# Sums of squares of loaded weight units, two to four slots later

## The chip, the cores and the metric

The kernel runs on one core of a Trainium2 chip. The metric is the time of one execution on the device in microseconds (us): 822.87 us, the median of 3 runs (822.29 to 823.02).

## The reference, cut to what matters

One decoder layer over 512 tokens of width 2048. The input is normalised and multiplied with a matrix of 2048 x 7168; its columns feed a convolution (value and gate), q, k and v of an attention, and two gates. Both branches meet in an output projection.

```python
h = rms_norm(x, norm_g)
z = h @ w_in
a_val, a_glu, a_gate, q, k, v, b_gate = jnp.split(z, SPLIT_POINTS, axis=-1)
...
y = jnp.concatenate([y_a, y_b], axis=-1) @ w_out
return x + y
```

All of it is computed in fp32; the kernel reaches that with three 16-bit products, from a high and a low part of each operand.

## The kernel before, in words

**Units and groups.** The weights are cut into groups of 512 columns, in the order of GROUPS: vg0, vg1, vg2, vg3 (value and gate of the convolution), q0, k0, v0, bg0, q1 and so on. A group of the input projection is four units of 512 rows (1 MB each): vg2 is units 8 to 11, vg3 12 to 15, q0 16 to 19, k0 20 to 23, v0 24 to 27, bg0 28 to 31, q1 32 to 35. The first two groups are computed in another way (exact_matmuls). Eight buffers (RING) hold raw units. When a unit is done with, the load of the unit eight further on is issued on SP's queue (load, L256).

**What is done to a unit.** A loaded unit is first measured (measure, L267): ScalarE (ACT) squares its 2048 columns and sums them (row_squares, L188). When the four units of a group are measured, `bound` (L192) makes the group's scale from the sums: a ones-matmul on TensorE, a reduce on VectorE (DVE), two small instructions on GpSimd (POOL), and, two slots later, two more on DVE. With the scale, ACT writes the high part of a weight in 16 bits and DVE the low part. Four buffers (PARTS) hold such parts, so a new part waits until TensorE is done with the part four before it.

**Two kinds of groups.** A plain unit is split whole (split_hi L296, split_lo L301), and takes eight slots of six matmuls over 512 columns. The three groups in SEVEN (vg3, q0, v0) are computed with seven products in place of eight, of blocks of half the columns, each product in four slots of twelve matmuls over 256 columns: 28 slots for four units (input_products, L1103). The seven products want the blocks a11, a22, a12 and a21 of the weights and four sums of them. The sums s2, s3 and s4 are made in the raw buffers by DMAs that POOL issues and that accumulate (`add`, L1119), s1 by DVE. For each product, in the order of `order`, `hi` puts the high part five slots and `lo` (L1125 and below) the low part four slots ahead of the product's slots, for each of two pairs of units. The products in order are a22, a11, a12, s3, s1, s2, s4 (in vg3 a11 is before a22); product n runs in slots 4n to 4n+3, pair 0 in the first two of them.

**What sets the order.** The program is written out slot by slot. `after(n, fn)` puts work on a calendar n ticks later; the clock counts eight ticks a unit, and in a group of seven it jumps one tick after every seven slots, since 28 slots stand for 32 ticks. What is due in a slot is issued before that slot's own parts, and both before its matmuls. Every engine runs its instructions in that order; one that waits holds up all behind it. DVE also carries the convolution, a few instructions a slot up to a pace (run_conv, L850).

**The squares.** In a group of seven, `lo` gives a raw buffer free when its last sums are split: in slots 12, 20, 20 and 22. It then loads the unit eight further on, and measures it MEASURE ticks later:

```python
raw.pop(i0 + j)
load(i0 + j + RING)
after(MEASURE, lambda j=j: measure(i0 + j + RING))
```

Before, with MEASURE = 8, the four squares of k0's units stand in slots 19, 27 and 27 of vg3 and slot 1 of q0; those of v0's units in the same slots of q0 and k0; those of q1's in the same slots of v0 and bg0. A plain unit measures the unit eight further on nine ticks after its own split: those of q0's units in slots 6 of unit 8, 3 of unit 9, 3 of unit 10 and 3 of unit 11, those of bg0's in slot 5 of unit 20 and slots 3 of units 21, 22 and 23. In slot 3 of units 11 and 23 `hi` also puts the first high part of the next group of seven, behind the square.

Of the kernel before, what the change touches and what calls it, by code (L numbers as in the profile page):

```python
# [27 lines left out]
RING = 8  # L28
# [24 lines left out]
SEVEN = (("vg", 3), ("q", 0), ("v", 0))  # L53
# [2 lines left out]
SUM_FROM = 58  # L56
SUM_STEP = 10
PACE_2 = 1480
MEASURE = 8
IN_W1 = [g for g in GROUPS if g[0] in ("vg", "q", "k", "v", "ag", "bg")]  # L60


# [22 lines left out]
def layer(ctx: ExitStack, tc: tile.TileContext, xt, w1, w2, w3, g_in, conv_w, conv_b,  # L85
# [34 lines left out]
    def after(n, fn):  # L120

        calendar.setdefault(clock[0] + max(n, 1), []).append(fn)
# [65 lines left out]
    def row_squares(src, acc, n, scale=1.0):  # L188
        with nc.allow_low_precision(reason="a bound"):
            A.activation(junk[:, :n], src, AF.Square, scale=scale, accum_out=acc)  # L190

    def bound(name, sums, done, top=TOP):  # L192


        bufs = 8 if name == "w" else 1
        scale = small.tile([P, 1], F32, name=f"{name}s", bufs=bufs)
        inv = small.tile([P, 1], F32, name=f"{name}i", bufs=bufs)
        n = sums.shape[-1]

        def sum_up():  # L200
            ps = s_ps.tile([P, S], F32, name="ps_s")
            T.matmul(ps[:, 0:n], ones16, sums, start=True, stop=True)
            V.tensor_reduce(scale, ps[:, 0:n], axis=AX.X, op=OP.add)
            G.tensor_scalar(scale, scale, 1e-30, 2.0 ** (-2 * top), op0=OP.max, op1=OP.mult)  # L204
            rsqrt(scale)

        def finish():
            pow2_floor(scale)
            V.reciprocal(inv, scale)
            done(scale, inv)  # L210

        after(2, sum_up)
        after(4, finish)
# [27 lines left out]
    units = []  # L241
# [14 lines left out]
    def load(i, cuts=(0, KU)):  # L256
        if i < len(units):
            w, g, p = units[i][:3]
            raw[i] = raw_pool.tile([P, KU, S], F32, name="wf")
            for a, b in zip(cuts, cuts[1:]):  # L260
                load_part(i, a, b)
# [5 lines left out]
    def measure(i):  # L267
        if n_exact <= i < len(units):
            group = units[i][3:]
            mine = of_group[group]  # L270
            j = mine.index(i)
            if group not in sums:
                sums[group] = small.tile([P, len(mine)], BF16, name="wsum")
                to_measure[group] = len(mine)
            row_squares(raw[i].rearrange("p k n -> p (k n)"), sums[group][:, j:j + 1], KU * S)
            to_measure[group] -= 1
            if not to_measure[group]:
                after(4, lambda: bound("w", sums.pop(group), lambda s, v: wscale.update({group: (s, v)}),
                                       TOP - (group[0] == "wa" or group in SEVEN)))
# [16 lines left out]
    def split_hi(i):  # L296
        if i < n_plain:
            parts[i] = [part_pool.tile([P, KU, S], F16, name=n, tag="part") for n in ("wh", "wl")]
            A.activation(parts[i][0], raw[i], AF.Copy, scale=wscale[units[i][3:]][0])  # L299

    def split_lo(i):  # L301
        if i < n_plain:
            wh, wl = parts[i]
            V.scalar_tensor_tensor(wl, raw.pop(i), wscale[units[i][3:]][0], wh, op0=OP.mult, op1=OP.subtract)
            load(i + RING)
            after(9, lambda: measure(i + RING))

    def split16(src, scale, name):

# [793 lines left out]
    def input_products(i0):  # L1103
# [23 lines left out]
        def lo(name, pair):  # L1127
# [3 lines left out]
            for j in range(4):  # L1131
                mine = ("s2", "s4") if j % 2 else ("s1", "s3")
                if all((n, j // 2) in done for n in mine) and all(m in free for m in range(j)) and j not in free:
                    free.add(j)
# [4 lines that stand above are left out]
# [153 lines left out]
    def startup(n):  # L1292

        s, second = divmod(n, 2)
        todo = []
        if not second:
            if s + 3 < KU * n_exact:
                todo += [lambda: exact_hi(s + 3), lambda: exact_lo(s + 3)]
            if s + 2 < KC:
                todo.append(lambda: split_x(s + 2))  # L1300
        if n == 0:
            for k in range(1, KC):
                after(4 + (k - 1) * 26 // 14, lambda k=k: square_x(k))
            for n in range(KC):
                after(NORM_FROM + n * (70 - NORM_FROM) // KC, lambda k=n // 2 + 4 * (n // 8) + 4 * (n % 2): norm_x(k))
            for j in range(8):
                after(SUM_FROM + SUM_STEP * j // 2, lambda j=j: sum_x(j))
            g = token_rsqrt(xacc, D, RMS_EPS, rstd, rrow)
            for m in (32, 33, 36):
                after(m, lambda: next(g, None))  # L1310
            for m, fn in ((21, x_consts), (40, score_consts), (37, u_consts)):
                after(m, fn)
            after(8 * n_exact - 4, lambda: split_hi(n_exact))
            after(8 * n_exact - 3, lambda: split_lo(n_exact))
        return todo
# [6 lines left out]
    for i in range(n_plain):  # L1322
        kind, g = group = units[i][3:]
        if group in SEVEN:
            if i == of_group[group][0]:
                plan = ahead.pop(i) + later
                later = []
                n_next = i + 4
                if units[n_next][3:] in SEVEN:
                    ahead[n_next] = input_products(n_next)  # L1330
                    plan += [(n + 28, fn) for n, fn in ahead[n_next] if n < 0]
                else:
                    plan = [(24, lambda: split_hi(n_next)), (25, lambda: split_lo(n_next))] + plan
                for n in range(28):
                    clock[0] = 8 * i + n + n // 7
                    for fn in due_now():
                        fn()
                    first = [fn for k, fn in plan if k == n]
                    for fn in first[:]:
                        if fn.__name__ != "matmuls":  # L1340
                            fn()
                    run_conv()
                    for fn in first:
                        if fn.__name__ == "matmuls":
                            fn()
                later = [(n - 28, fn) for n, fn in plan if n >= 28]
                if units[n_next][3:] not in SEVEN:
                    for n, fn in later:
                        after(8 * n_next + n - clock[0], fn)
                    later = []  # L1350
                if kind == "k":
                    attention(g)
            continue
        exact = i < n_exact
        if exact:
            order = [(None, None)] * 8
        else:
            order = [(m, hf) for m in range(4) for hf in range(2)]
            extra = [[] for _ in range(8)]
            if i == n_plain - 1:  # L1360
                for n, fn in seven_parts(0):
                    if n < 0:
                        extra[n].append(fn)
            if i + 1 < len(units) and units[i + 1][3:] in SEVEN:
                ahead[i + 1] = input_products(i + 1)
                for n, fn in ahead[i + 1]:
                    if n < 0:
                        extra[n].append(fn)
            else:
                extra[0].append(lambda: split_hi(i + 1))  # L1370
                extra[2].append(lambda: split_lo(i + 1))
            if i + 1 < len(units) and units[i + 1][3] == "wb":
                for m in range(2):
                    extra[4 * m].append(lambda m=m: fetch_res(2 * units[i + 1][4] + m))
# [77 lines left out]
```

## Time and profile before

| | |
|---|---|
| median of 3 runs | 822.87 us |
| the profiled execution | 823.61 us |
| its span, first to last instruction | 821.8 us |
| TensorE busy | 809.5 us, 98% |
| VectorE (DVE) busy | 706.4 us, 86% |
| ScalarE (ACT) busy | 553.9 us, 67% |
| GpSimd (POOL) busy | 140.3 us, 17% |
| granted clock of TensorE | full speed in all slices |

All times are us from the start of the span of one profiled execution. Matmuls are pipelined and their ends are modelled, so the start of one to the start of the next is their cost, not the recorded length. Idle time of an engine counts where another engine waits for it in the end. Lines are those of the kernel; many DVE instructions are recorded under one helper (L80), and are told apart by what they write and read: `ws` is a part in a group of seven, `wh` and `wl` the parts of a plain unit, `junk` the squares, `wf` a raw unit.

### The profile page before, as it was taken

Reading aid. Unit: us, or ns where it says so; the run is one execution under the profiler, and the core shown is the slowest. Engines: PE = TensorE matmul, PEld = TensorE weight load, DVE = VectorE, ACT = ScalarE, POOL = GpSimd, SP = SyncE. Lnnn points to the kernel's source line nnn. Section 1 sums busy time; section 2 is a strip of 40 time slices with the busy share of each in tenths; the row PEclk is TensorE's granted clock in tenths of the full one; section 3 lists DMA queues with packets and bytes.
Section 4 is the critical chain, followed back from the end, with each engine's and each line's share of the span. In section 5 each row is a group of like instructions: output and inputs, shape, how many; then the busy total and the mean of one; then the engine's idle time right before and its main releaser. Section 6 shows DMA issues by size and latency. Waiting matters only on the chain.

```text
span 821.8 us, 13494 instructions
## 1 busy us (share of the span) xinstructions
PE 809.5 (98%) x5271; PEld 501.3 (61%) x5271; DVE 706.4 (86%) x1181; ACT 553.9 (67%) x778; POOL 140.3 (17%) x159
## 2 busy tenths in 40 slices
PE   9999999999998999999999999999999999999998
PEld 6787645878644864444444444444444444788887
DVE  6768989968887979999999988997667798998985
ACT  6667687475744589577665849577688858766540
POOL 0001020413043600002304010001110002422420
PEclk9999999999999999999999999999999999999999
DMA  9852343995583873737474641636343377578752
GB/s 339 340 215 100 105 114 93 146 255 114 219 180 85 147 242 103 167 103 167 128 137 129 170 131 55 163 103 167 103 116 103 119 232 249 111 176 187 133 104 65
DMA packets 98625, 125.62 MB, mean 153 GB/s; under 512 B 62720, under 2 KB 83968, under 8 KB 89344
## 3 DMA queue, kind: packets, MB, share of 16 engines
q1 hardware_dynamic: 80800, 107.38, 42.2%
q0 software_dynamic: 17472, 17.30, 15.0%
q8 instruction: 41, 0.67, 0.3%
q14 instruction: 24, 0.20, 0.1%
q10 hardware_dynamic: 288, 0.07, 0.0%
HBM read 88.56 MB, written 4.19 MB: 113 GB/s over the span
## 4 chain that ended last, share of the span: by engine, by line
PE 71%; DVE 17%; DMA 5%; issue 3%; ACT 3%; POOL 1%; SPq 0%; ACTq 0%; DVEq 0%; POOLq 0%
PE ps_l L408 17%; PE ps_l L409 17%; PE ps_l L410 17%; PE ps_l L876 10%; DVE cv L80 6%; DMA wf<-w_dram 4%; DVE wl L80 3%; PE ps_s L410 2%; PE ps_s L408 2%; PE ps_s L409 2%; DVE ws L80 2%; PE ps_s L720 2%; PE ps_o L760 2%; DMA wf<-wf 1%; ACT junk L190 1%
## 5 line engine op out<-in xcount | busy, mean ns | idle before, releaser
L80 DVE SCALAR_TENSOR_TENSOR cv<-u,cw,cv 128x511 f32<-128x511 f32 (+14 forms) x240 | 162.4, 727 | 0.0
L190 ACT ACTIVATE junk<-wf 128x2048 uint8<-128x2048 f32 x68 | 129.2, 1900 | 26.6 <-DMA wf<-w_dram 26.3
L408 PE MATMUL ps_l<-x,wh 128*128 128x512 f16 x320 | 121.3, 379 | 0.3 <-DVE glu L80 0.3
L299 ACT ACTIVATE wh<-wf,ws 128x2048 f16<-128x2048 f32 x44 | 87.7, 1993 | 50.3 <-PE ps_l L409 50.3
L410 PE MATMUL ps_l<-x,wl 128*128 128x512 f16 x320 | 121.3, 379 | 0.0
L409 PE MATMUL ps_l<-x,wh 128*128 128x512 f16 x320 | 121.3, 379 | 0.0
L80 DVE SCALAR_TENSOR_TENSOR wl<-wf,ws,wh 128x2048 f16<-128x2048 f32 x45 | 105.6, 2346 | 8.9 <-ACT wh L299 8.9
L80 DVE SCALAR_TENSOR_TENSOR ws<-wf,ws 128x1024 f16<-128x1024 f32 x70 | 89.0, 1278 | 17.9 <-ACT ws L1125 15.6
L409 PE MATMUL ps_l<-wl,x 128*128 128x512 f16 x256 | 97.0, 379 | 0.5 <-DVE wl L80 0.5
L408 PE MATMUL ps_l<-wh,x 128*128 128x512 f16 x256 | 97.1, 379 | 0.0
L410 PE MATMUL ps_l<-wh,x 128*128 128x512 f16 x256 | 97.0, 379 | 0.0
L408 PEld LDWEIGHTS <-wh 128*128 128x128 f16 x480 | 47.0, 98 | 55.2 <-issue 3.5
L410 PEld LDWEIGHTS <-wl 128*128 128x128 f16 x480 | 46.9, 98 | 53.6 <-DVE wl L80 0.4
L409 PEld LDWEIGHTS <-wh 128*128 128x128 f16 x480 | 46.9, 98 | 50.4 <-issue 0.7
L876 PE MATMUL ps_l<-xr,wr 128*128 128x512 f32 x288 | 70.2, 400 | 0.1
L204 POOL TENSOR_SCALAR ws<-ws 128x1 f32<-128x1 f32 x22 | 9.3, 424 | 331.2 <-DVE ws L80 302.3
L876 PEld LDWEIGHTS ps_l<-xr,wr 128*128 128x128 f32 x288 | 54.5, 190 | 14.1 <-ACT xr L335 1.0
L410 PEld LDWEIGHTS <-x 128*128 128x128 f16 x352 | 34.4, 98 | 33.4 <-issue 2.0
L408 PEld LDWEIGHTS <-x 128*128 128x128 f16 x352 | 34.4, 98 | 32.4 <-issue 1.9
L409 PEld LDWEIGHTS <-x 128*128 128x128 f16 x352 | 34.4, 98 | 30.4 <-issue 0.4
L943 ACT ACTIVATE ws<-wf,ws 128x1024 f16<-128x1024 f32 x28 | 32.1, 1147 | 28.5 <-PE ps_l L410 9.6
L1125 ACT ACTIVATE ws<-wf,ws 128x1024 f16<-128x1024 f32 x42 | 46.4, 1137 | 3.8 <-PE ps_l L410 2.5
(250 smaller groups left out, 1826.2 us busy)
## 6 DMA issues: line engine op xcount, KB each, us to landing
wf<-w_dram SPq DMA_DIRECT2D x72, 1024.0 KB, 5.2
wf<-wf POOLq DMA_DIRECT2D x30, 512.0 KB, 6.3
x<-xt_dram SPq DMA_DIRECT2D x16, 256.0 KB, 6.7
res<-xt_dram SPq DMA_DIRECT2D x8, 512.0 KB, 6.8
out_dram<-res SPq DMA_DIRECT2D x15, 256.0 KB, 2.2
wf<-w_dram SPq DMA_DIRECT2D x7, 512.0 KB, 7.2
wf<-wf POOLq DMA_DIRECT2D x6, 256.0 KB, 6.2
qk<-qhl SPq DMA_TRANSPOSE x40, 3.1
```

Source lines behind the costliest of these rows:

```text
L80: return getattr(self.engine, name)(out, src, *args, **kw)
L190: A.activation(junk[:, :n], src, AF.Square, scale=scale, accum_out=acc)
L204: G.tensor_scalar(scale, scale, 1e-30, 2.0 ** (-2 * top), op0=OP.max, op1=OP.mult)
L299: A.activation(parts[i][0], raw[i], AF.Copy, scale=wscale[units[i][3:]][0])
L408: T.matmul(ps, ah, bh, start=first, stop=False)
L409: T.matmul(ps, ah, bl, start=False, stop=False)
L410: T.matmul(ps, al, bh, start=False, stop=last)
L720: T.matmul(ps[i, a], qk["q", hf][q][rows, p4, i * P:w], qk["k", hf][k][rows, p4, :w], start=n == 0, stop=n == 2)
L760: T.matmul(po[rows, i * P:(i + 1) * P], vs[hf][j // 2][:, j % 2, 2 * p4 + a, vp * DH:(vp + 1) * DH], got["t", a][:, pp * (ALL // P) + FROM ...
L876: T.matmul(banks[group, m], wt[:, a, m * P:(m + 1) * P], xk[b], start=k == 0 and a == b == 0, stop=k == KC - 1 and a == 1)
L943: A.activation(t[:, 0], block(name), AF.Copy, scale=wscale["wa", g][0])
L1125: A.activation(t[:, 0], block(name, pair), AF.Copy, scale=wscale[group][0])
```

## The change

A constant goes from 8 to 12, so that the squares which the groups of seven put on the calendar come four ticks later (three or four slots: vg3's in slot 22 and in slots 2, 2 and 5 of q0, and likewise for the two other groups). And `split_lo` of a plain unit, where the next group is one of the three groups of seven, measures 11 ticks later instead of 9: units 8 to 11 (they measure 16 to 19) and 20 to 23 (they measure 28 to 31). Unit 31's square then stands in slot 5 of unit 23. What follows from the last square of a group, the bound, moves with it. No instruction is added or taken away.

```diff
-MEASURE = 8
+MEASURE = 12
...
+    def of_next(i):
+        return units[min(i + 4, len(units) - 1)][3:]
+
     def split_lo(i):
         if i < n_plain:
             wh, wl = parts[i]
             V.scalar_tensor_tensor(wl, raw.pop(i), wscale[units[i][3:]][0], wh, op0=OP.mult, op1=OP.subtract)
             load(i + RING)
-            after(9, lambda: measure(i + RING))
+            after(11 if of_next(i) in SEVEN else 9, lambda: measure(i + RING))
```

## Rows read from the trace of the kernel before

**Rows 1.** The page: the span, and the busy time of TensorE (PE) and of its weight loads (PEld) with the other engines'.
```profile
span 821.8 us, 13494 instructions
PE 809.5 (98%) x5271; PEld 501.3 (61%) x5271; DVE 706.4 (86%) x1181; ACT 553.9 (67%) x778; POOL 140.3 (17%) x159
```

**Rows 2.** Busy time of each engine by stretch. Columns: the stretch, its length, then busy us and number of instructions for PE, PEld, DVE, ACT and POOL, the granted clock, the share of the DMA engines, GB/s. vg3 and q0 lie in the first two stretches, k0 in the third, v0 in the fourth.
```profile
139.00:176.00 37.00, 36.38 (x333) 32.25 (x332) 30.07 (x37) 21.70 (x23) 10.88 (x10) 1.00 0.84 172
176.00:215.00 39.00, 37.60 (x344) 33.34 (x342) 35.07 (x44) 24.61 (x27) 10.49 (x10) 1.00 0.65 151
215.00:257.00 42.00, 41.52 (x196) 18.88 (x195) 35.78 (x50) 22.85 (x23) 10.97 (x11) 1.00 0.68 185
257.00:299.00 42.00, 37.85 (x339) 32.88 (x338) 34.96 (x42) 28.86 (x34) 19.67 (x16) 1.00 0.74 162
```

**Rows 3.** The waits of TensorE from 299 us to the end: who waited for whom, us in total, times, the longest.
```profile
PE ps_s L565 <- DVE lnacc L80: 0.8, 1, 0.8
```

**Rows 4.** The timeline of TensorE: start, length, line, what it writes and reads, its shape, and in brackets the idle time before it and what ended it. The first two are neighbours without a wait, the first of them the first of slot 24 of vg3; the other nine are all with a wait from 139 to 299 us.
```profile
170.71 0.27 PE L408 MATMUL ps_l<-x,ws 128*128 128x256 f16 x1
170.82 0.27 PE L409 MATMUL ps_l<-x,ws 128*128 128x256 f16 x1
...
171.72 0.28 PE L410 MATMUL ps_l<-x,ws 128*128 128x256 f16 x1 [0.62 <-DVE ws L80]
...
180.82 0.27 PE L409 MATMUL ps_l<-ws,tx 128*128 128x256 f16 x1 [1.18 <-DVE ws L80]
...
194.40 0.27 PE L409 MATMUL ps_l<-ws,tx 128*128 128x256 f16 x1 [0.22 <-DVE ws L80]
...
216.12 0.38 PE L409 MATMUL ps_l<-wl,x 128*128 128x512 f16 x1 [0.48 <-DVE wl L80]
...
258.65 0.27 PE L408 MATMUL ps_l<-ws,tx 128*128 128x256 f16 x1 [1.12 <-ACT ws L1125]
...
259.97 0.27 PE L409 MATMUL ps_l<-ws,tx 128*128 128x256 f16 x1 [1.05 <-DVE ws L80]
...
265.46 0.27 PE L408 MATMUL ps_l<-ws,x 128*128 128x256 f16 x1 [0.18 <-ACT ws L1125]
...
266.79 0.27 PE L409 MATMUL ps_l<-ws,x 128*128 128x256 f16 x1 [1.05 <-DVE ws L80]
...
278.31 0.27 PE L409 MATMUL ps_l<-ws,tx 128*128 128x256 f16 x1 [0.75 <-DVE ws L80]
```

**Rows 5.** The waits of ACT and of DVE from 97 to 299 us, the largest ones that this text uses: us in total, times, the longest.
```profile
ACT junk L190 <- DMA wf<-w_dram: 23.0, 8, 5.8
...
DVE ws L80 <- ACT ws L1125: 15.6, 8, 5.6
DVE ws L80 <- POOL ws L168: 4.0, 3, 2.5
```

**Rows 6.** The timelines of ACT and of DVE around the squares of unit 20 (167.30) and of unit 31 (255.56), with the idle time before an instruction in brackets. `sq` is a square of a tile of k.
```profile
167.30 1.91 ACT L190 ACTIVATE junk<-wf 128x2048 uint8<-128x2048 f32 x1 [5.14 <-DMA wf<-w_dram]
...
169.21 4.25 ACT L1125 ACTIVATE ws<-wf,ws 128x1024 f16<-128x1024 f32 x4
...
253.28 0.69 ACT L507 ACTIVATE sq<-ps_l,esc 128x512 f32<-128x512 f32 x1 [5.98 <-DVE z L80]
255.56 1.91 ACT L190 ACTIVATE junk<-wf 128x2048 uint8<-128x2048 f32 x1 [1.59 <-DMA wf<-w_dram]
...
170.37 1.28 DVE L80 SCALAR_TENSOR_TENSOR ws<-wf,ws 128x1024 f16<-128x1024 f32 x1 [5.59 <-ACT ws L1125]
...
258.63 1.28 DVE L80 SCALAR_TENSOR_TENSOR ws<-wf,ws 128x1024 f16<-128x1024 f32 x1 [3.45 <-ACT ws L1125]
```

**Rows 7.** The chain of waits from 155 to 182 us, in order of time: start, length, the piece. The DMA is the load of unit 20, from its issue to its landing.
```profile
157.27 10.00 DMA wf<-w_dram
...
180.82 0.27 PE ps_l L409
```

**Rows 8.** From issue to landing: the loads issued from 155 to 300 us (17 of them), the one issued at 171.69 us by itself, and POOL's accumulating DMAs issued from 155.4 to 158.4 us (3 of them).
```profile
DMA to landing us min/median/max: 4.9/6.6/11.9
...
DMA to landing us min/median/max: 4.9/4.9/4.9
...
DMA to landing us min/median/max: 6.3/14.6/15.5
```

**Rows 9.** The timelines of POOL and DVE around the bound of q0, from 141.83 us, and its neighbours: L204 and L168 are POOL's two instructions of a bound (those at 114.67 and 114.98 are of the bound before), the DMA at 145.31 and the one behind it make the sum s2 for the two pairs; then DVE's low parts, its sum s1 of the second pair, and the first low part of s1.
```profile
114.67 0.23 POOL L204 TENSOR_SCALAR ws<-ws 128x1 f32<-128x1 f32 x1 [30.39 <-DVE ws L80]
114.98 0.56 POOL L168 TENSOR_TENSOR ws<-ws,half 128x1 f32<-128x1 f32 x1
...
141.83 1.19 POOL L204 TENSOR_SCALAR ws<-ws 128x1 f32<-128x1 f32 x1 [22.82 <-DVE ws L80]
143.10 1.46 POOL L168 TENSOR_TENSOR ws<-ws,half 128x1 f32<-128x1 f32 x1
...
145.31 2.68 POOL L1119 DMA_DIRECT2D wf<-wf  x2 [0.27 <-issue]
...
141.65 2.47 DVE L80 SCALAR_TENSOR_TENSOR ws<-wf,ws 128x1024 f16<-128x1024 f32 x2
...
154.17 1.22 DVE L80 TENSOR_TENSOR wf<-wf 128x1024 f32<-128x1024 f32 x1 [0.68 <-DMA wf<-wf]
...
155.97 1.27 DVE L80 SCALAR_TENSOR_TENSOR ws<-wf,ws 128x1024 f16<-128x1024 f32 x1
```

## The prediction, on record before the result

> **What bounds the kernel now.** I read the page first: TensorE is busy 98% of the span [rows 1]. So a change of order can only give back TensorE's own pauses, or make new ones. The second view is the busy time by stage [rows 2]: from 139 us to 299 us TensorE is idle 0.62 + 1.40 + 0.48 + 4.15 = 6.65 us, and from 299 us on its only wait for another engine is 0.8 us [rows 3]. Third, the timeline of TensorE shows where those 6.65 us lie: nine pauses, four from 171 to 217 us (0.62, 1.18, 0.22, 0.48) and five from 258 to 279 us (1.12, 1.05, 0.18, 1.05, 0.75), all at a weight's high or low part made by ScalarE (ACT) or VectorE (DVE) [rows 4]. The reader should see that a pause costs more than its idle: a 128x256 matmul is recorded as 0.27 long, while the next starts 0.11 later (170.71, 170.82). So each pause costs 0.16 more: 2.50 + 4 x 0.16 = 3.1 us in the first cluster, 4.15 + 5 x 0.16 = 5.0 us in the second, 8.1 us together. That is what this change can reach, 1.0% of the time.
>
> Fourth, the waits say who is late. In 97 to 299 us ACT waited 23.0 us for loads to land, always in front of a sum of squares, and DVE waited 15.6 us for ACT's high parts [rows 5]. Fifth, the timelines tie these together. The square of unit 20 sits in ACT's queue in front of the high parts of the last product, waits 5.14 us and starts when its load lands; four high parts then run in a row, and DVE stands idle 5.59 us for the first of them. At 255.56 the square of unit 31 does the same: 1.59 us on ACT, 3.45 us on DVE [rows 6]. The chain of waits confirms it: load, square, high part, low part, and then a matmul, at 180.82 [rows 7].
>
> **The change, part by part.** No instruction is added or removed; twenty squares (1.9 us on ACT each) move, with what is timed from the last of each group: a ones-matmul on TensorE, a reduce on DVE, two instructions on GpSimd (POOL), then two small ones on DVE. On TensorE that ones-matmul stands five or six slots behind its last square, as before, so it does not come to wait for ACT. One slot of a group of seven is twelve matmuls of 0.11, so 1.31 us [rows 4]. Loads, transposes and accumulating DMAs keep their place in the queues of SP and POOL relative to each other.
>
> *Squares of units 20 to 23 (MEASURE), beside groups vg3 and q0.* Unit 20's goes from slot 19 of vg3 to slot 22; 21 and 22 from slot 27 to slot 2 of q0; 23 from slot 1 to slot 5. Slot 24 of vg3 begins at 170.71 [rows 4], so slot 18, from where the buffer of the first high part of s4 is free, begins at 162.8. ACT has been idle since 162.2 (167.30 - 5.14) [rows 6], and with the square out of the way that part runs at 162.8 instead of 169.21, its low part ends by 165.5, and slot 24 needs it at 170.8. The pause of 0.62 goes, and so do the 5.59 us of DVE. With them goes 1.18 at 180.82: DVE ran without a gap behind its stall and made that low part late. Slot 22 begins at 168.1; the load landed at 167.27 (157.27 + 10.00) [rows 7], so ACT hardly waits, or, if the load is 2 us later, holds up only parts that are needed from slot 0 of q0 on.
>
> *The price of that in q0.* Squares 21 and 22 stand in slot 2, in front of the high part of a12, which the third product needs in slot 8. From slot 2 on: two squares 3.8, high part 1.14, low part 1.28: 6.2 us, 4.8 slots. Cover: 6 slots. Square 23 then stands in front of the second half, with 10 slots to its need; ACT has four high parts (4.6), three squares (5.7) and about 1 us of small work from slot 0 to there, and DVE then a low part (1.28): 12.6 us, 9.6 slots, an estimate from the lengths in [rows 6]. I cost it at 0; if the cover is gone, each us later is one us lost (a rival below).
>
> *The pauses 0.22 and 0.48* come at the end of the same full stretch of DVE: 35.07 us busy of 39 from 176 to 215 us [rows 2], with a pace of side work that leaves it a few per cent, so the 5.59 us were never made up. With the stall gone DVE is early there. First cluster: 3.1 us back.
>
> *Squares of 24 to 27 (MEASURE), in q0 and k0*, move the same way, past the split of unit 21. The plain group k0 asks for one split in eight slots, so nothing there waits. Their bound moves from just before DVE's low part of unit 22 to behind it; DVE had waited 4.0 us in three places for POOL's part of a bound [rows 5]. This helps load 30, which waits for that low part. SP's transposes and load 31, behind it in SP's queue, follow sooner.
>
> *Squares of 28 to 31 (the second hunk).* Unit 31's moves from in front of the first high part of v0 to in front of the second. That first part then waits for nothing but ACT itself, free at 253.97 (253.28 + 0.69) [rows 6]. It ends by 255.2 and its low part by 256.6; TensorE wanted them 0.27 - 0.11 + 1.12 before 258.65, at 257.4. So 1.12 and 1.05 go, and DVE gets most of its 3.45 us, with which 0.75 at 278.31 goes. For 0.18 and 1.05 at 265 to 267 us I give half: that high part's buffer is in use until v0 begins, and it also queues behind the squares of k's last tile. Second cluster: 5.0 - 0.6 = 4.4 us.
>
> *Squares of 16 to 19 (the second hunk) and the bound of q0.* The squares move by two slots among work with no pause behind it: 0. The bound moves from slot 1 to slot 3 of vg3, still in front of the POOL-issued sums s2, which now wait for it later. TensorE reaches the ones-matmul at 143.2 (21 slots before 170.71), the reduce follows at about 144.3, POOL's two instructions take from 0.23 + 0.56 to 1.19 + 1.46, and the DMA starts at 145.1 to 147.0, against 145.31: between 0.2 earlier and 1.7 later [rows 9]. DVE's sum s1 waits for that DMA already (0.68 at 154.17), and the low part behind it ends at 157.24 where slot 16 needs it at 160.2. Slack 3.0, so 0 on the path even at the upper end, which is the row from the same place.
>
> POOL and DVE get in each other's way there: the same POOL instruction took 0.56 us at 114.98 and 1.46 at 143.10, beside low parts of DVE; but two of those low parts together took 2.47 us, no more than elsewhere [rows 9]. So the rows show POOL held up, which the 1.7 holds, and DVE not. The Trainium skill, "SBUF — State Buffer", section "Who interferes with whom", speaks against the move: a DVE instruction with two SBUF inputs and a GpSimd one that reads SBUF shut each other out, and whichever starts second waits for the whole of the first. By that rule DVE may be the one that waits, and the sum would be 6.2 instead of 7.5 (third rival); the two low parts speak against it here.
>
> *Squares of 32 to 35 (MEASURE), in v0 and bg0.* They pass out of the way of the last high parts of v0, where TensorE did not pause after 278.31 [rows 4]: 0 either way, bounded by the same high parts' slack of four slots.
>
> **Sum.** 3.1 + 4.4 = 7.5 us back, 0 paid. The profiled execution took 823.61 us around a span of 821.8, which is 0.74 above the median of 822.87, so I take the difference to the median: 822.87 - 7.5 = 815.4 us. Ends: all 8.1 back and a few tenths of waiting elsewhere gives 814.3; only the pauses directly behind a square (next part) 818.3.
>
> **Rivals.** *Half of it.* DVE is full in these stretches [rows 2], so pauses later in a stretch may come from its own load, not from the stall before. Then only 0.62, 1.18, 1.12 and 1.05 go: 3.97 + 4 x 0.16 = 4.6, time 818.3. For it: DVE idles little anywhere from 176 to 257 us. Against: from 139 to 170 us a group of the same build ran without one pause [rows 4].
> *The wait only moves.* If loads land late enough that the squares still wait in their new places, in front of other high parts, the pauses stay: 822.9. For it: in 155 to 173 us loads and POOL's copies landed 10.0 to 15.5 us after their issue [rows 7, 8]. Against: the load issued at 171.69 took 4.9 [rows 8].
> *The bound of q0 is late.* If DVE stands still while POOL's two instructions run, s1 is late by 1.7 + 1.19 + 1.46 = 4.3 us against a slack of 3.0: a pause of 1.3 us at slot 16 of vg3, 6.2 us back instead of 7.5, time 822.87 - 6.2 = 816.7. For it: POOL's 1.46. Against: DVE's 2.47 [rows 9].
> *Slower.* The same lateness of loads, but deciding in q0. If load 22, issued at 171.69 as before, took 15.5 us like the slowest copy there [rows 8], it would land at 187.2; square, high and low part end at 191.5, where the third product begins at 188.7 (170.71, twelve slots, and pauses of 0.8 and 1.4 [rows 4]). That is 2.8 us of new pause with none won: 825.7. It decides once that load lands after about 184. Against: DVE no longer stalls before it, so the load goes out earlier.
>
> **How the numbers follow.** This kernel's runs can tell some 0.2%, 1.6 us, from no change. Forecast 0.65, half 0.18, late bound 0.03, moved wait 0.08, slower 0.06. So faster by over 0.2%: 0.65 + 0.18 + 0.03 = 0.86; within: 0.08; slower: 0.06. The predicted time is the forecast's. The range reaches from all pauses gone with 0.5 us to spare, 813.8, past the half case to 819.4.
>
> **What would show it.** Right: TensorE's nine pauses gone but for some tenths near slots 4 and 5 of v0; ACT's waits for loads in this stretch down from 23.0 to under 8; DVE's for high parts from 15.6 to under 5; TensorE's busy time the same 809.5. Wrong: a pause at the third product of q0 or at s1 of vg3; a square that still waits 5 us for its load; or unchanged pauses at the tail of q0 with no DVE stall before them, which would make DVE's load their cause.

## The result

The changed kernel takes **817.75 us** (median of 4 runs, 817.56 to 817.90) beside 822.94 us for the kernel before on the same chip (4 runs, 822.29 to 823.68): a ratio of 0.9936, 95% interval [0.9919, 0.9954]. Faster by 5.2 us, as forecast in sign, 2.4 us above the predicted 815.4 and inside the range. The profiled execution took 817.56 us around a span of 815.8. Three executions of the whole study ran far longer than the others of their kernel (1413.04 us with the square later, 842.85 and 1713.92 us for the kernel before), and ratios and intervals leave them out.

The page of the changed kernel, its first line and that of busy time. Lines after line 298 stand three higher than before, so L408, L409 and L1125 of before are L411, L412 and L1128 here.

```profile
span 815.8 us, 13495 instructions
PE 807.9 (99%) x5271; PEld 500.6 (61%) x5271; DVE 707.1 (87%) x1181; ACT 553.6 (68%) x778; POOL 138.1 (17%) x159
```

Against [rows 1] the same work stands in a shorter span. Of TensorE's 1.6 us less busy time, 1.0 is the extra 0.16 that each of six vanished pauses had left in the records; the rest, 0.6, lies in front of unit 8 (95.67 us busy there against 96.25), where this execution was 0.65 us ahead before the first instruction that the change moves.

Busy time by stretch in the changed kernel, columns as in [rows 2]:

```profile
139.00:176.00 37.00, 37.00 (x342) 33.12 (x341) 33.78 (x42) 20.72 (x22) 10.86 (x9) 1.00 0.87 193
176.00:215.00 39.00, 39.00 (x347) 33.61 (x345) 34.36 (x43) 25.35 (x28) 9.69 (x9) 1.00 0.70 170
215.00:257.00 42.00, 41.98 (x211) 20.40 (x210) 36.26 (x51) 26.00 (x27) 12.98 (x15) 1.00 0.59 150
257.00:299.00 42.00, 39.77 (x337) 32.23 (x336) 37.73 (x50) 27.67 (x30) 15.18 (x13) 1.00 0.83 201
```

Where [rows 2] had 0.62, 1.40, 0.48 and 4.15 us of idle, only the last stretch has some left, 2.2 us. The timeline of TensorE shows where; these are all its waits for another engine from 139 to 299 us:

```profile
259.45 0.27 PE L411 MATMUL ps_l<-ws,x 128*128 128x256 f16 x1 [0.35 <-ACT ws L1128]
260.77 0.27 PE L412 MATMUL ps_l<-ws,x 128*128 128x256 f16 x1 [1.05 <-DVE ws L80]
272.39 0.27 PE L412 MATMUL ps_l<-ws,tx 128*128 128x256 f16 x1 [0.74 <-DVE ws L80]
```

They are the last three of [rows 4] (265.46, 266.79 and 278.31 there, 6 us earlier here); the other six are gone. The waits of ACT and DVE from 97 to 299 us, which answer to [rows 5]:

```profile
DVE wl L80 <- ACT wh L299: 6.8, 5, 2.6
DVE ws L80 <- ACT ws L1128: 4.9, 6, 1.2
...
DVE ws L80 <- POOL ws L168: 1.8, 2, 1.0
...
ACT junk L190 <- DMA wf<-w_dram: 1.3, 1, 1.3
```

ACT's waits for loads fell from 23.0 to 1.3 us, DVE's for high parts in the groups of seven from 15.6 to 4.9. Those for high parts of plain units (`wh`) grew from 2.8 us in the kernel before to 6.8; the longest, 2.55, ends at 289.39, behind the last pause. How that came about at unit 20 is in the timelines of ACT and then of DVE, answering to [rows 6]:

```profile
162.41 1.15 ACT L1128 ACTIVATE ws<-wf,ws 128x1024 f16<-128x1024 f32 x1 [0.90 <-PE ps_l L413]
165.03 1.15 ACT L1128 ACTIVATE ws<-wf,ws 128x1024 f16<-128x1024 f32 x1 [1.47 <-PE ps_l L413]
167.50 1.91 ACT L190 ACTIVATE junk<-wf 128x2048 uint8<-128x2048 f32 x1 [1.32 <-DMA wf<-w_dram]
...
169.41 2.17 ACT L1128 ACTIVATE ws<-wf,ws 128x1024 f16<-128x1024 f32 x2
...
164.41 1.28 DVE L80 SCALAR_TENSOR_TENSOR ws<-wf,ws 128x1024 f16<-128x1024 f32 x1
...
166.92 1.28 DVE L80 SCALAR_TENSOR_TENSOR ws<-wf,ws 128x1024 f16<-128x1024 f32 x1
...
170.58 1.28 DVE L80 SCALAR_TENSOR_TENSOR ws<-wf,ws 128x1024 f16<-128x1024 f32 x1 [1.07 <-ACT ws L1128]
```

The two high parts of s4 now run at 162.41 and 165.03 instead of 169.21 and behind, and DVE's 5.59 us became 1.07: a high part of q0 still stands behind the square, which still waits 1.32 us. That 1.07 matters below.

**A second ruler.** Counting the matmuls of each unit in the trace gives the start of every unit's first product. The table has these starts against the kernel before, in us, each less its own value at unit 12 (-0.67 to 0 in these runs, and within 0.01 the same at unit 8, before any moved instruction). A tap is one step of the convolution on DVE. vg3 is units 12 to 15, q0 16 to 19, k0 20 to 23, v0 24 to 27.

| kernel | unit 16 | 20 | 24 | 29 | 63 |
|---|---|---|---|---|---|
| the change | -0.80 | -2.60 | -4.53 | -5.41 | -5.38 |
| own groups alone | -0.79 | -2.59 | -4.35 | -4.48 | -4.45 |
| units ahead alone | +1.32 | +1.25 | -0.04 | -0.81 | -0.79 |
| convolution held | -0.80 | -2.60 | -4.53 | -8.08 | +3.96 |
| no wait for loads | -0.80 | -2.60 | -4.53 | -6.51 | -6.50 |
| held, then faster | -0.80 | -2.60 | -4.53 | -7.94 | -1.04 |
| bound of q0 later | -0.80 | -2.60 | -4.53 | -6.63 | -6.58 |
| 7 taps moved too | -0.79 | -2.59 | -4.52 | -6.24 | -5.52 |
| 9 taps moved too | -0.80 | -2.60 | -4.53 | -8.47 | -5.88 |
| 9 taps, in time | -0.79 | -2.59 | -4.53 | -8.46 | -7.41 |

### The profile page after: what moved, and what is told of

It reads as the page before. It is cut to its first block, busy times and chain, and to the rows that moved or that the text cites. A ratio compares the mean times of both kernels' runs of the same rounds, so it can differ in the third digit from the quotient of the medians.

```text
span 815.8 us, 13495 instructions
## 1 busy us (share of the span) xinstructions
PE 807.9 (99%) x5271; PEld 500.6 (61%) x5271; DVE 707.1 (87%) x1181; ACT 553.6 (68%) x778; POOL 138.1 (17%) x159
## 4 chain that ended last, share of the span: by engine, by line
PE 69%; DVE 19%; ACT 5%; issue 3%; DMA 3%; POOL 1%; SPq 0%; ACTq 0%; DVEq 0%; POOLq 0%
PE ps_l L411 17%; PE ps_l L412 17%; PE ps_l L413 16%; PE ps_l L879 10%; DVE cv L80 6%; DVE wl L80 3%; DVE ws L80 3%; ACT junk L190 2%; PE ps_s L413 2%; PE ps_s L411 2%; PE ps_s L412 2%; PE ps_s L723 2%; PE ps_o L763 2%; DMA wf<-w_dram 1%; DVE cb L80 1%
## 5 line engine op out<-in xcount | busy, mean ns | idle before, releaser
L411 PE MATMUL ps_l<-x,wh 128*128 128x512 f16 x320 | 121.4, 379 | 0.3 <-DVE glu L80 0.3
L412 PE MATMUL ps_l<-x,wh 128*128 128x512 f16 x320 | 121.3, 379 | 0.0
L411 PE MATMUL ps_l<-wh,x 128*128 128x512 f16 x256 | 97.1, 379 | 0.0
L412 PE MATMUL ps_l<-wl,x 128*128 128x512 f16 x256 | 97.1, 379 | 0.0
L411 PEld LDWEIGHTS <-wh 128*128 128x128 f16 x480 | 47.0, 98 | 55.4 <-issue 3.5
L412 PEld LDWEIGHTS <-wh 128*128 128x128 f16 x480 | 46.9, 98 | 50.4 <-issue 0.7
L204 POOL TENSOR_SCALAR ws<-ws 128x1 f32<-128x1 f32 x22 | 10.7, 485 | 341.8 <-DVE ws L80 313.0
L411 PEld LDWEIGHTS <-x 128*128 128x128 f16 x352 | 34.4, 98 | 32.4 <-issue 1.9
L412 PEld LDWEIGHTS <-x 128*128 128x128 f16 x352 | 34.4, 98 | 30.6 <-issue 0.5
L1128 ACT ACTIVATE ws<-wf,ws 128x1024 f16<-128x1024 f32 x42 | 46.4, 1138 | 6.1 <-PE ps_l L413 3.9
```

The costliest lines, as they stand in the source:

```text
L411: T.matmul(ps, ah, bh, start=first, stop=False)
L412: T.matmul(ps, ah, bl, start=False, stop=False)
L1128: A.activation(t[:, 0], block(name, pair), AF.Copy, scale=wscale[group][0])
```

## The experiments

My theory after the result: each hunk (the constant for the groups' own squares, the longer wait for the units ahead of a group) took away the pauses behind its own squares, because ACT no longer waits for a load with high parts queued behind it; what is left in v0 is DVE's lag, made by something else. The rival for what is left: unit 31's square still stands in front of v0's second high part, 1.9 us long.

**The changed kernel again**.

> The changed kernel as it is, so that the other runs of this call have it beside them on the same chip. 817.7 us; three pauses of TensorE before 300 us, at 259.5, 260.8 and 272.4 us, 2.1 us of idle.

Measured: 817.44 us (817.28 to 817.91), ratio 0.993 [0.9917, 0.9942].

**One hunk at a time.** Each is the kernel with the other hunk undone:

```
own groups alone:   -MEASURE = 8       +MEASURE = 12      (line 309: after(9, ...) again)
units ahead alone:   MEASURE = 8       +after(11 if of_next(i) in SEVEN else 9, ...)
```

> Only the four slots of the groups of seven: squares of units 20 to 27 and 32 to 35 later, those of 16 to 19 and 28 to 31 at their old places. Theory (each hunk takes away the pauses of its own squares): the pauses of 171 to 217 us go (3.1 us), those at 258.7 and 260.0 us stay, 819.8 us. Rival (all of the lateness is carried over from the first place to the later ones): this hunk alone gives the whole gain, 817.7 us, and no pause at 258.7 us.

> Only the two slots of the units ahead of a group of seven: squares of units 16 to 19 and 28 to 31 later, the others at their old places. Theory (each hunk takes away its own pauses): four pauses between 171 and 217 us stay, the waits of ScalarE for unit 20 and its neighbours stay near 17 us, and the two pauses at 258.7 and 260.0 us go, 2.5 us: 820.5 us. Rival (all comes from the groups' own squares): no gain, 822.9 us. Rival (unit 31's square is as much in the way two slots later): 822.5 us or more.

Measured: 818.89 us, ratio 0.9946 [0.9934, 0.9958], for the groups' own squares; 822.08 us, 0.9986 [0.9977, 0.9995], for the units ahead. In the table the two gains, 4.45 and 0.79, add up to 5.24 of the 5.38. The split is not the one I expected, though. The own-groups hunk also took the pause of 1.12 ahead of v0, which I had put down to unit 31's square. What is left there is the neighbour of that pause, in TensorE's timeline, and the last three of [rows 4]:

```profile
255.33 0.27 PE L409 MATMUL ps_l<-ws,tx 128*128 128x256 f16 x1 [1.05 <-DVE ws L80]
```

The other hunk alone first loses 1.3 us in vg3, then wins 2.1 from unit 20 on. That loss is in the timelines of TensorE and of ACT of this kernel:

```profile
171.15 0.28 PE L411 MATMUL ps_l<-x,ws 128*128 128x256 f16 x1 [0.84 <-ACT ws L1128]
172.47 0.28 PE L413 MATMUL ps_l<-x,ws 128*128 128x256 f16 x1 [0.93 <-DVE ws L80]
...
168.05 1.91 ACT L190 ACTIVATE junk<-wf 128x2048 uint8<-128x2048 f32 x1 [6.46 <-DMA wf<-w_dram]
```

The bound of q0 is two slots later, so GpSimd's sums, s1 behind them and load 20 behind the low parts of s1 are late, and the square of unit 20, still at its old place, waits 6.46 us instead of 5.14. The size is the one that my third rival put on a late bound (1.3 us), but by luck: that rival had DVE stand still and a pause at slot 16, and here a load came late. In the full change TensorE doesn't feel it near there, because nobody asks for load 20 before its square at slot 22.

**DVE's lag or the square?** First the lag taken away:

```
 def run_conv():
+    if 178 <= clock[0] < 194:
+        return
```

(the counter that paces the convolution isn't drained meanwhile, so its next step is emitted only in slot 218), and then the square moved:

```
-after(11 if of_next(i) in SEVEN else 9, ...)
+after(17 if i == 23 else 11 if of_next(i) in SEVEN else 9, ...)
```

> The changed kernel with VectorE's convolution held back for 16 slots ahead of the products of v0 (it goes on from there). Theory 1 (what is left at 259 to 273 us is VectorE's lag, because twelve convolution steps lie in front of the first evacuation of k, which then reaches ScalarE 3 us late): the pauses at 259.5 and 260.8 us go, 1.7 us, 816.0 us, and with the one at 272.4 us 815.1 us. Theory 2 (unit 31's square of 1.9 us lies in front of the second high part of a22, whenever the evacuations come): the pauses stay, 817.7 us. Theory 3 (VectorE is simply full there): the work held back comes in front of low parts of v0 and the pauses are as large or larger, 817.7 to 820 us.

> The changed kernel with the square of unit 31 six slots later still, behind the second high part of a22 and those of a11 of v0. Theory 1 (what is left at 259 to 273 us is VectorE's lag; holding the convolution back took it away, so the square's place does not matter): the three pauses stay, 817.5 us. Theory 2 (the square's 1.9 us lies in the path as well): the second high part of a22 comes 1.9 us earlier, the low part behind it 1.2 us earlier, and the pauses at 259.5 and 260.8 us (0.35 and 1.05 us, 1.7 us with what each adds) go: 815.8 us.

Measured: with the convolution held 827.57 us, ratio 1.0052 [1.0038, 1.0065]; with the square later 817.71 us, 0.9938 [0.9924, 0.9951], no different from the changed kernel (no trace of it is read here, so which pauses it has isn't shown). So six slots more for the square bring nothing. The convolution's work on DVE does: in the table the held kernel is 2.7 us further ahead at unit 29, and of the three pauses one of 0.22 us is left. How the lag reaches TensorE in the changed kernel, by the timelines of DVE and then of ACT:

```profile
241.06 7.73 DVE L80 SCALAR_TENSOR_TENSOR cv<-u,cw,cv 128x491 f32<-128x491 f32 x12
248.71 0.74 DVE L80 SCALAR_TENSOR_TENSOR z<-ps_l,esc,qg 128x512 f32<-128x512 f32 x1
...
255.06 1.28 DVE L80 SCALAR_TENSOR_TENSOR ws<-wf,ws 128x1024 f16<-128x1024 f32 x1 [1.24 <-ACT ws L1128]
...
259.43 2.48 DVE L80 SCALAR_TENSOR_TENSOR ws<-wf,ws 128x1024 f16<-128x1024 f32 x2 [1.16 <-ACT ws L1128]
...
249.49 0.69 ACT L510 ACTIVATE sq<-ps_l,esc 128x512 f32<-128x512 f32 x1 [10.78 <-DVE z L80]
...
258.26 3.21 ACT L1128 ACTIVATE ws<-wf,ws 128x1024 f16<-128x1024 f32 x3
```

Twelve convolution steps stand in front of the first evacuation of k (z); ACT, idle for 10.78 us, waits for it with v0's high parts behind it in its queue; and DVE then waits for those. In the held kernel, the same place on DVE:

```profile
246.62 0.75 DVE L80 SCALAR_TENSOR_TENSOR z<-ps_l,esc,qg 128x512 f32<-128x512 f32 x1 [5.11 <-PE ps_l L413]
```

Here DVE waits for TensorE instead. The price comes 350 us later, in the timeline of TensorE of the held kernel, where pw's products read the convolution:

```profile
609.08 1.05 PE L392 MATMUL ps_s<-ones,lnacc 128*128 128x2 f32 x8 [2.61 <-DVE lnacc L80]
613.56 1.22 PE L405 MATMUL ps_s<-diag,ones 128*128 128x512 f32 x2 [1.76 <-DVE diag L80]
618.36 0.58 PE L411 MATMUL ps_l<-u,wh 128*128 128x512 f16 x1 [3.58 <-ACT u L314]
619.87 0.58 PE L412 MATMUL ps_l<-u,wh 128*128 128x512 f16 x1 [0.92 <-DVE u L80]
```

These wait for the late normalization. The last two are recorded at 0.58 where [rows 4] has 0.38 for that shape, and the granted clock from 612 to 624 us is 0.50 in this kernel: behind the first waits TensorE ran at the lower of its two levels, 1.2 instead of 2.4 GHz, which is a part of the 12.0 us lost from unit 29 to unit 63.

**Was it the wait for loads at all?** The kernel before, with the squares where they were:

```
+if 16 <= i < 36:
+    row_squares(ones[:, None, :].to_broadcast(...), ..., scale=0.02)
```

> The kernel before, every square at its old place, but those of units 16 to 35 read a block of ones that lies in SBUF from the start, in place of the loaded weights (the bounds of these units, and with them the output, are left out of the computation). Same length of work on ScalarE, same order, no wait for a load. Theory A (the pauses came from ScalarE's wait for loads, in whose shadow the high parts lay): the pauses at 171 to 217 us go, as in the changed kernel, and of those at 259 to 278 us as many as there: 817.5 us. Theory B (it was the 1.9 us of work ahead of the high parts, whatever its data): all pauses stay within 0.3 us, 823 us.

Measured: 817.10 us, ratio 0.9928 [0.9916, 0.9941]. Theory A holds for seven of the nine pauses: the same 1.9 us of work in the same order, without the wait, takes all away up to 260 us and leaves two in v0, 0.72 and 0.75. It is 1.1 us ahead of the change at unit 29. The 1.3 us wait for load 20 is one thing that the change still has and this kernel hasn't; the places of the squares and bounds differ too.

**Paying the convolution back, and the bound of q0.**

```
held, then faster:   the hold above        -PACE_2 = 1480   +PACE_2 = 1540
bound of q0 later:  -after(11 if of_next(i) in SEVEN else 9, ...)
                    +after(15 if of_next(i) == SEVEN[0] else 11 if of_next(i) in SEVEN else 9, ...)
```

> The changed kernel with the convolution held back for 16 slots ahead of v0 and then given 1540 in place of 1480 per slot while attention runs, so that its last tap comes in slot 400 as in the changed kernel (415 with the hold alone). Theory 1 (the loss of the hold alone was the convolution's late end, 10 us of waits at the products that read it, and no more): the three pauses before 273 us are gone or at most one of 0.2 us is left, no waits near 610 us, 815.1 us. Rival (VectorE, 96 percent busy from 299 to 500 us, has no room for the taps that moved): new pauses between 299 and 560 us, 817.5 us or more.

> The changed kernel with the squares of units 16 to 19 four slots later still, so the bound of q0 six slots later than before instead of two. Theory (the bound of q0 has slack behind it: what it delays is the sums that GpSimd issues and with them load 20, and nobody waits for load 20 before its square at 167.5 us): POOL's sums up to 5 us later only if they stand behind it, no new pause over 0.5 us, 817.5 to 818.2 us. Rival (the sums of s2 come late enough to reach the low parts of s1 and s4 of vg3, as in the run with the two slots alone): a pause of 1 to 4 us between 155 and 172 us, 818.5 to 821.5 us.

Measured: 821.06 us, ratio 0.9981 [0.9972, 0.999], and 816.62 us, 0.9925 [0.9912, 0.9937]. The first bears the rival out: 7.9 us ahead at unit 29, 6.9 of it lost again, in pauses such as these of TensorE, in attention and at the convolution's end; behind the second the granted clock was 0.72 from 550 to 556 us:

```profile
484.33 0.18 PE L202 MATMUL ps_s<-ysumb,ones 128*128 128x4 bf16 x1 [1.79 <-DVE st L80]
...
550.13 1.16 PE L568 MATMUL ps_s<-lnacc,ones 128*128 128x512 f32 x2 [2.68 <-DVE lnacc L80]
```

The second beat its own expectation, neither theory having foreseen a gain. GpSimd around the bound of q0 in the changed kernel, answering to [rows 9], then in this one:

```profile
143.20 1.19 POOL L204 TENSOR_SCALAR ws<-ws 128x1 f32<-128x1 f32 x1 [24.09 <-DVE ws L80]
144.47 0.57 POOL L168 TENSOR_TENSOR ws<-ws,half 128x1 f32<-128x1 f32 x1
145.00 2.68 POOL L1122 DMA_DIRECT2D wf<-wf  x2
```

```profile
142.26 1.33 POOL L1122 DMA_DIRECT2D wf<-wf  x1 [20.84 <-DVE ws L80]
144.78 1.30 POOL L1122 DMA_DIRECT2D wf<-wf  x1 [1.19 <-DVE ws L80]
148.66 0.65 POOL L204 TENSOR_SCALAR ws<-ws 128x1 f32<-128x1 f32 x1 [2.58 <-DVE ws L80]
149.39 0.92 POOL L168 TENSOR_TENSOR ws<-ws,half 128x1 f32<-128x1 f32 x1
```

With the bound out of their way the two sums of s2 start 2.7 and 1.6 us earlier, on a clock 0.4 us later by the table's unit 12. Load 20, issued at 157.25 as in the changed kernel (157.24), lands after 9.3 us instead of 10.2, at 166.55, in time for its square, and DVE's low part behind that no longer waits. That the earlier sums made the load faster is an argument from their order; no run separates the two. The timelines of ACT and of DVE in this kernel:

```profile
166.57 1.91 ACT L190 ACTIVATE junk<-wf 128x2048 uint8<-128x2048 f32 x1
...
169.66 1.28 DVE L80 SCALAR_TENSOR_TENSOR ws<-wf,ws 128x1024 f16<-128x1024 f32 x1
```

No pause goes away near there. DVE did 34.80 us of work from 139 to 176 us instead of 33.78. Instruction by instruction, with unit 12 as zero, DVE is 0.35 us ahead of the changed kernel in front of this wait, 1.35 behind it and still 1.23 at 272 us. So the lead lasts until v0, where the pauses shrink from 0.35, 1.05 and 0.74 to 0.52 and 0.75: 1.2 us by the table. The 1.1 us of the kernel without waits for loads fits.

**Both together.** To the kernel with the later bound, a pause of the convolution in chosen slots, its counter drained as usual, and a small raise of pace:

```
 7 taps:           183 <= clock[0] < 186 or 191 <= clock[0] < 196    PACE_2 = 1500
 9 taps:           182 <= clock[0] < 187 or 191 <= clock[0] < 200    PACE_2 = 1500
 9 taps, in time:  182 <= clock[0] < 187 or 191 <= clock[0] < 200    PACE_2 = 1510
```

> The kernel with the squares of units 16 to 19 four slots later still, in which VectorE's convolution also pauses in slots 183 to 185 and 191 to 195 and is then given 1500 in place of 1480 per slot (last tap in slot 401, as before in 400). Theory 1 (VectorE's lag ahead of v0 makes the two pauses that are left, 0.52 and 0.75 us, 1.6 us with what each adds; seven taps, 4.6 us of VectorE, are more than the lag): at least the first goes, and 815.0 to 815.9 us. Rival (attention's stretch has no room even for seven taps): new pauses after 300 us eat the gain, 816.6 us or more.

> As the run beside it, with slots 182 to 186 and 191 to 199 (last tap in slot 405, the wait of the normalization for attention ends in slot 429 instead of 426). Theory 1: both pauses of v0 go, 815.0 us, and up to 1 us comes back where the products read the convolution. Rival (attention's stretch has no room): slower than the run with fewer taps moved, 817 us or more.

Measured: 817.61 us, ratio 0.993 [0.9916, 0.9943], and 817.77 us, 0.9934 [0.9921, 0.9946]. The first failed where I expected it to work: at unit 29 it is 0.4 us behind the kernel without the hold, with pauses of 1.15 and 0.75 in v0. Taps moved by only a few slots come back in front of other low parts, as the timelines of its DVE and then of TensorE show:

```profile
246.40 0.75 DVE L80 SCALAR_TENSOR_TENSOR z<-ps_l,esc,qg 128x512 f32<-128x512 f32 x1 [2.26 <-PE ps_l L413]
...
263.53 1.34 DVE L80 SCALAR_TENSOR_TENSOR cv<-u,cw,cv 128x485 f32<-128x485 f32 x2
...
267.12 1.28 DVE L80 SCALAR_TENSOR_TENSOR ws<-wf,ws 128x1024 f16<-128x1024 f32 x1
...
268.45 0.27 PE L412 MATMUL ps_l<-ws,x 128*128 128x256 f16 x1 [1.15 <-DVE ws L80]
```

DVE waits for TensorE at z here, as in the held kernel, so it is no longer late there; the taps behind z make the pause. The second cleared v0, gained 1.8 us there, and lost 2.6 later, 1.7 of it at pw where the normalization ends three slots later. So last:

> The run with nine taps moved out of the way of v0 (8.5 us ahead of before at 300 us, 2.4 us of it lost again between 545 and 625 us), with 1510 in place of 1500 per slot, so that the last tap is in slot 401 and the normalization's wait ends in slot 426, as in the changed kernel. Theory 1 (1.6 us of the loss was the later end of the normalization): the waits at 613 us go and 0.9 us of loss stays, 816.2 us. Rival (attention's stretch has no room for the taps at whatever pace): the loss moves to pauses before 560 us, 817.5 us or more.

> The kernel with the squares of units 16 to 19 four slots later still, once more, beside the run above on the same chip: 816.6 us (theory: the gain over the changed kernel's 817.4 to 817.7 us is there in every run of it; rival: it was the start of that one run, 817.5 us).

Measured: **815.59 us** (815.43 to 815.69), ratio 0.9907 [0.9893, 0.9921], and 816.42 us, 0.9918 [0.9904, 0.9932]. The kernel with the later bound took 816.14 to 817.04 us in its ten runs, the changed kernel 817.28 to 817.91 in nine: no overlap. The last version is the fastest of the study. It has no pause in v0, and the one wait of TensorE from 140 to 640 us is this:

```profile
546.85 1.12 PE L568 MATMUL ps_s<-lnacc,ones 128*128 128x512 f32 x2 [1.72 <-DVE lnacc L80]
```

0.9 us of what it wins is lost there; the changed kernel waits 0.8 at this line, which points to attention not leaving DVE quite enough room for nine taps.

## Why the prediction was right, and where it was off

- **What bounds the kernel** was right: the loads in front of the squares were the cause of seven of the nine pauses (the run without waits for loads), and the pauses were all there was to win. With all nine gone the count is 8.5 us against my 8.1.
- **The first cluster, 3.1 us:** measured 3.27 (unit 21, just behind the pause of 0.48). The pauses of 0.22 and 0.48 went too, so DVE's stall, not its own load, had made them; the "half" rival fails here.
- **The price in q0, 0:** no pause at its third product; the load of the slower rival didn't come late, and the wait for loads didn't move to the new places (1.3 us in all). "ACT hardly waits" at slot 22 was 1.32 us, and "holds up only parts that are needed from slot 0 of q0 on" was true of TensorE, but DVE lost 1.07 us there and did not get them back before v0. I had priced a wait by the pause behind it and missed this one. It was not the only one: in q0, DVE waits for ACT, in whose queue the squares of units 21 and 22 run from 177.89 to 181.82, and the timeline of DVE in the changed kernel has

```profile
182.25 0.42 DVE L80 TENSOR_TENSOR u<-cb 128x256 f32<-128x256 f32 x1 [1.80 <-ACT cb L1222]
183.29 1.28 DVE L80 SCALAR_TENSOR_TENSOR ws<-wf,ws 128x1024 f16<-128x1024 f32 x1 [0.62 <-ACT ws L1128]
```

Neither square waited for its load, so this is what their own 1.9 us cost DVE. No run takes these two waits away.

- **The second cluster, 4.4 us: the step that failed.** Measured 5.41 - 3.27 = 2.1. 1.12 and 1.05 went, as said. Of 0.18 and 1.05 I gave half (0.6; with 0.16 for each pause it is 0.8), and 0.75 I let go because "DVE gets most of its 3.45 us"; 0.35, 1.05 and 0.74 stayed. The reason was in the views that I read: DVE is 35.78 of 42 us busy ahead of v0 [rows 2], and the square of k at 253.28 waited 5.98 us for DVE's z [rows 6]. I read the lag as caused by the stall alone, and so as gone with it. With unit 12 as zero, DVE is 5.3 us earlier than before at 164.41, but only 3.15 at the first z (248.71; 252.51 in the kernel before), and TensorE is 3.24 earlier itself by unit 22: DVE comes to v0 no further ahead of TensorE than it was. What makes it late is the convolution's work in front of z and of v0's low parts (the held run, -8.08 at unit 29, and those with nine taps) and 1.1 to 1.2 us of the old wait at load 20 (the run with the later bound). For this cluster my "half" rival was the right reading.
- **Unit 31's square as the cause of 1.12** was half wrong: the own-groups hunk alone takes that pause away. The other hunk is worth 0.9 us on top of it, 1.05 at 255.33 in that kernel, and six further slots bring nothing.
- **The bound of q0, 0 on the path:** GpSimd's first DMA stands at 145.00 in the changed kernel and 0.65 us later, at 145.65, on the clock of before: 0.3 us late, in the range of -0.2 to 1.7. That costs no pause in the change but 1.3 us without the other hunk. The bigger matter, that the bound has no business in front of the sums, I didn't see: moving it behind them is worth 1.2 us.
- **GpSimd and DVE in each other's way.** In the changed kernel GpSimd's 143.20 took 1.19 us while a low part of DVE ran (143.03 to 144.31), and its next, with none of DVE's low parts beside it, 0.57; DVE's low part kept its 1.28. The Trainium skill, "SBUF — State Buffer", section "Who interferes with whom", says that the one which starts second waits; the trace agrees, and the second one here was GpSimd. My rival needed DVE to be the second.

## What to carry to other kernels

In a queue that runs in order, an instruction that waits for a load belongs behind the work whose data is already there; here a few slots were enough, and the price was paid in slack of its own result and in waits of the engine behind it. On an engine that is nine tenths busy a wait is not forgiven because no pause follows it: here 1.1 us lost on VectorE at 170 us came back as 1.2 us of pauses at 260 us, so follow such an engine's lead over the bound engine, not only the pauses. Work moved off a full stretch must land where there is room, and for the whole of it: seven taps moved by a few slots gained nothing, nine moved past v0 gained 1.8 us and gave 1.0 back.

## What was not expected of the hardware

GpSimd's 128x1 power instruction took 0.57 us in the changed kernel, with DVE idle. In the kernel before it took 1.46, with a low part of DVE beside it for the first 1.02 (to 144.12) [rows 9], and in the one with the later bound 0.92 (149.39), with a convolution step beside it for the first 0.49 (to 149.88). Behind DVE's end it took 0.44 and 0.43 more, so its length went with what DVE did meanwhile, while DVE's own instructions kept theirs. Three executions of the instruction show this; no run was made for it.
